# A planner's spare time behind the landing of projection weights, and the bytes it counts for a gate's rows

## The chip, the cores and the metric

The kernel runs on one core of a Trainium2 chip. The metric is the device time of one execution in microseconds (us), taken as the median of several runs. A profile of one execution shows what each engine did: PE (matrix products, with PEld for its weight loads), ACT, DVE and POOL (elementwise work), and SP, which here issues nearly every DMA.

## What is computed

One decoder block on 1024 tokens of width 1024, float32:

```python
mod = silu(c) @ w_ada + b_ada                    # 6 x 1024: shift, scale, gate for each half
h = rms_norm(x, g_attn_pre) * (1 + sc_a) + sh_a
proj = h @ w_in                                  # q, k, v of two mixers; part of q and k is rotated
oa = banded_attention(qa, ka, va, 127, sink)     # mixer A: 8 query heads on 2 key heads, window 128
ob = dilated_mixture_attention(qb, kb, vb)       # mixer B: 8 heads, three dilated windows
mixed = concat(rms_norm(oa, g_mix_a), rms_norm(ob, g_mix_b))
x = x + gt_a * rms_norm(mixed @ w_out, g_attn_post)
h = rms_norm(x, g_mlp_pre) * (1 + sc_m) + sh_m
x = x + gt_m * rms_norm(square(relu(h @ w_up)) @ w_down, g_mlp_post)
```

`gt_a` and `gt_m` are the two gates: one row of 1024 numbers each.

## The kernel before

**Products in three parts.** Each float32 operand is split into a high part (a cast on ACT) and a low part (a subtraction on DVE or POOL), and each product is three matrix products: high by high, high by low, low by high (L920, L921, L923 for the projections).

**Units.** The projection's columns are cut into six units, numbered 0 to 5 (two for mixer A, four for mixer B). A unit has three column groups `c` of 128, two halves `x` of the tokens, and eight slices `k` of the depth. Its weights come as six tiles of 128 x 512 floats (256 KB). Unit 0 is loaded in a fixed order during the start. For units 1 to 5 ("from unit two on", counted from one) `next_unit_w` makes, for each tile, a load (`load_w`, L541, tile `w_st`, two buffers) and a split (`split_w`): the cast on ACT (L550, into `w_hl`, six buffers) and the subtraction on DVE or POOL (L555), which gives the raw buffer back. Tiles one and two hold the first column group's slices 0 to 3 and 4 to 7, tiles three and four the second group's, five and six the third's. The next unit's loads are made when the second half of the unit before begins.

**Attention.** While units 1 to 5 are projected, the attention of the heads that are ready runs beside them: scores on PE (`s_ps`, L1203 and L1258), row minima on DVE (`mn`, L1222 and L1273), exponentials on ACT (`p_sb`, L1229 and L1278), a reciprocal on DVE (`den`), the normalisation on POOL or ACT (L1234, L1290), transposes on PE (`pt_ps`), the split of the transposed probabilities (`ph`, L1322 on ACT and L1326 on DVE), the product with v on PE (`o_ps`, L1338 to L1350). Projected q and k go out of `hl` into `qt` and `kt` by DMAs issued on SP (L863). After the attention come the output projection (`y_ps`) and the MLP (`mlp_ps`).

**Gates.** `ada_piece` makes pieces of the later modulation rows: it loads slices of `w_ada` (`wa_st`), accumulates them on POOL (24 pieces beside the attention) or DVE (8 pieces in the MLP), and after each fourth piece sums over the partitions on PE (`ada_ps`). For a gate (g = 0, 1 beside the attention, g = 6, 7 in the MLP) it also loads two rows of 512 floats, each broadcast to all 128 partitions (`f_gl`, L1112 and L1113, tile `gate_st`), then adds and multiplies on DVE (L1118, L1124 or L1126) and stores the gate (L1128).

**The planner.** The order on each engine is not left to a queue at run time. While the program is built, `Sched.run` places every step with a counted duration: at each turn it takes, over all engines, the step that can start first. On one engine ties go to the lower priority number; among DMAs on SP what counts first is also the start, then the priority (stores of q and k −12, weight tiles −10 to −9.5, modulation pieces 20, a gate's rows 19). The instructions are emitted in that order, and at run time each engine goes through its own in order, each waiting for its semaphores. What the planner counts is thus no waiting time of its own; it only decides who stands behind whom.

A load on SP counts as follows: it occupies SP for 0.62 us, enters one DMA queue (`dma`) no sooner than 1.1 us after its start, takes `nbytes / 345e3` us of it, and has landed 0.8 us later. A step on another engine that needs it is ready at that time plus the load's `slack`. Until now `slack` was 3.0 us for loads of priority 15 to 24 while the projections run (`SLACK`, set to 0 when the output projection opens) and 0 for all others; the same spare time is also added to the start of such a load.

Of the kernel before, what the change touches and what calls it, by code (L numbers as in the profile page):

```python
# [134 lines left out]
def lat(a, b):  # L135

    if a == "PE" or b == "PE":
        return 0.2
    return 0.06 if a == "POOL" else 0.14
# [38 lines left out]
class Sched:  # L178
# [21 lines left out]
    def op(self, eng, dur, emit, deps=(), **kw):  # L200

        o = self.step(dur, emit, deps, **kw)
        o.alts = None
        if isinstance(eng, str):
            self.queue[eng].append(o)
        else:
            o.alts = dict(zip(eng, zip(dur, emit)))
            for e in eng:
                self.queue[e].append(o)
        return o.ev  # L210
# [7 lines left out]
    def ready(self, o, e):  # L218
        t = 0.0
        for d in o.deps:  # L220
            if d.t is None:
                return None
            x = d.t + lat(d.eng, e) + (0.0 if e == "SP" else d.slack)
            if x > t:
                t = x
        for r, n in o.takes:
            if n == 0:
                continue
            if len(r.free) < n:
                return None  # L230
            x = sorted(r.free)[n - 1]
            if x > t:
                t = x
        return t + self.spare(o) if e == "SP" else t

    def spare(self, o):

        return self.slack if 15 <= o.prio < 25 else 0.0

    def give_out(self, e, o, start):  # L240
        dur, emit = o.alts[e] if o.alts else (o.dur, o.emit)
# [91 lines left out]
def t_as(n):  # L333
    return 0.2 + 0.00083 * n


def t_dv(n):
    return 0.066 + 0.00104 * n
# [19 lines left out]
def hybrid_block(ctx: ExitStack, tc: tile.TileContext, x, positions, w_ada, b_ada, g_attn_post, w_in, w_out,  # L358
# [7 lines left out]
    op, pe_op = sc.op, sc.pe_op  # L366
# [27 lines left out]
    r_stg, r_w, r_wst, r_hl = Res(5), Res(WR), Res(WS), Res(0)  # L394
# [60 lines left out]
    def stage(name):  # L455
        if st.stgp is None:
            return ring_r(name)
        return st.stgp.tile([P, 1024], F32, name=name, tag="stg")

    def load(emit, nbytes, deps=(), takes=(), prio=5, gives=(), after=None, n=1):  # L460
        return op("SP", nbytes / (345e3 if prio > -500 else 370e3), emit, deps, takes=takes, prio=prio, gives=gives, after=after, n=n)

    def rsqrt_mean(dst, src, dep):
        box = []
# [36 lines left out]
    def in_turn(emit, nbytes, ring):  # L501

        before, mine = gone[0], Ev()
        gone[0] = mine

        def issued():
            mine.t = 0.0
        return load(emit, nbytes, [before], takes=[(ring, 1)], prio=pri(), after=issued)

    e_c = load(lambda: nc.sync.dma_start(head[:], consts[:, 0:HEAD]), 106496, prio=pri())  # L510
    wa_t, wa_e = {}, {}

# [23 lines left out]
    w_raw, w_rawe, w_hl, w_e = {}, {}, {}, {}  # L536

    def load_w(u, i, prio=None, deps=()):
        def emit():
            t = w_raw[u, i] = prp.tile([P, 512], F32, name="w_st", tag="w_st", bufs=WS)  # L540
            nc.sync.dma_start(t[:], w_in[6 * u + i])  # L541
        if prio is None:
            w_rawe[u, i] = in_turn(emit, 262144, r_wst)
        else:
            w_rawe[u, i] = load(emit, 262144, deps, takes=[(r_wst, 1)], prio=prio)

    def split_w(*a):
        def hi():
# [15 lines left out]
    for a, n in order0:  # L564
        if a == "x":
            load_x(n)
        elif a == "w":
            load_w(0, n)
        else:
            load_ada(a, n)  # L570
# [12 lines left out]
    e = op("ACT", 0.1, lambda: A.activation(cond[:], c_raw, AF.Exp, scale=-1.0), [e_c], prio=0)  # L583
# [32 lines left out]
    e = op("DVE", 4.2, f_turns, [e_pos, e_c], prio=1)  # L616

    def f_sin():
# [5 lines left out]
                prio=1)  # L624
# [150 lines left out]
    def tables_b():  # L775
# [12 lines left out]
       prio=8)  # L788
# [200 lines left out]
    def next_unit_w(u, deps=()):  # L989
        if u + 1 < 6:  # L990
            for i in range(6):
                load_w(u + 1, i, prio=-10 + i / 10, deps=deps)
                split_w(u + 1, i)
# [54 lines left out]
    def ada_piece(i, eng, accp, psum, r_ps, r_acc=None):  # L1048
# [9 lines left out]
        def f_acc():  # L1058
# [3 lines left out]
            for j in range(2):  # L1062
# [8 lines left out]
        e = op("DVE" if eng is V else "POOL", 1.2 if eng is V else 4.1, f_acc,  # L1071
               [el, ada.e], takes=[(r_acc or r_adacc, 1)] if jp == 0 else [], gives=[(r_stg, 1)], prio=9)
# [19 lines left out]
        if row and g > 5:  # L1092
# [7 lines left out]
            def f_al(eng):  # L1100
                return lambda: eng.tensor_tensor(hl[0][:, 1], acc[0][:, :512], hl[0][:, 0].bitcast(F32), ALU.subtract)
            e = op("ACT", t_as(512), f_ah, [e], takes=[(r_stg, 1)], prio=4)
            ada.e = e
            e = op("DVE", t_dv(512), f_al(V), [e], gives=[(r_acc or r_adacc, 1)], prio=4)
        ef = pe_op("fin", (0.46 if g > 5 else 0.86) if row else 0.45, f_fin, [e], takes=[(r_ps, 1)],
                   gives=[(r_stg if row and g > 5 else r_acc or r_adacc, 1)])
        if row:
            gate, gp = (gate_d[0], g_attn_post) if g < 2 else (gate_d[1], g_mlp_post)

            def f_gl():  # L1110
                ada.gate[g] = t = stage("gate_st")
                nc.sync.dma_start(t[:, 0:512], b_ada[0:1, col:col + 512].to_broadcast([P, 512]))  # L1112
                nc.sync.dma_start(t[:, 512:1024], gp[0:1, n0:n0 + 512].to_broadcast([P, 512]))  # L1113
            eg = load(f_gl, 524288, [e], takes=[(r_stg, 1)], prio=19)

            def f_g1():
                t = ada.gate[g]
                V.tensor_tensor(t[:, 0:512], b[0][:, :512], t[:, 0:512], ALU.add)  # L1118
            e1 = op("DVE", t_dv(512), f_g1, [ef, eg], gives=[(r_ps, 1)], prio=4)

            def f_g2():
                t = ada.gate[g]
                if g < 2:
                    V.tensor_tensor(t[:, 0:512], t[:, 0:512], t[:, 512:1024], ALU.mult)  # L1124
                else:
                    V.scalar_tensor_tensor(t[:, 0:512], t[:, 0:512], D ** 0.5, t[:, 512:1024], ALU.mult, ALU.mult)  # L1126
            e2 = op("DVE", t_dv(512), f_g2, [e1], prio=4)
            e_mod[g] = load(lambda: nc.sync.dma_start(gate[:, n0:n0 + 512], ada.gate[g][:, 0:512]), 262144, [e2],  # L1128
                            gives=[(r_stg, 1)], prio=18)
        else:  # L1130
            k0 = n0 // P

            def f_c():
                if g < 4:
                    V.tensor_tensor(s_m[:, k0:k0 + 4], b[0][:, 0:4], cols[:, 40 + k0:44 + k0], ALU.add)
                else:
                    V.tensor_tensor(g_m[:, k0:k0 + 4], b[0][:, 0:4], b1m[:, k0:k0 + 4], ALU.add)
                    V.tensor_tensor(g_m[:, k0:k0 + 4], g_m[:, k0:k0 + 4], cols[:, 16 + k0:20 + k0], ALU.mult)
            e_mod[g] = op("DVE", 0.15, f_c, [ef], gives=[(r_ps, 1)], prio=4)

    def feed_ada():
        if st.d > 1.0 + ada.i * 4.1 / NADA and ada.i < NADA:
            ada_piece(ada.i, G, lambda: adp.tile([P, 512], F32, name="ada_acc", tag="ada_acc", bufs=1), lambda: px.tile([P, 512], F32, name="ada_ps", tag="x"), r_x)
            ada.i += 1
        return ada.i == NADA
# [1052 lines left out]
    def feed_ada2():  # L2198
        if ada.i < 32:
            if ada.i >= NADA and ml.begun > 8 + 2 * (ada.i - NADA):  # L2200
                ada_piece(ada.i, V, lambda: stage("ada_acc"),
                          lambda: px.tile([P, 512], F32, name="ada_ps", tag="x"), r_x, r_stg)
                ada.i += 1
            return False

        def f_gate():
            ml.gate = ring_r("gate_m")
            nc.sync.dma_start(ml.gate[:], gate_d[1][:])
        ml.e_gate = load(f_gate, 524288, [e_mod[6], e_mod[7]], takes=[(r_h2, 1)], prio=17)
        return True  # L2210
# [32 lines left out]
```

## Time and profile before

| | us |
|---|---|
| median of 3 runs (lowest, highest) | 1120.49 (1119.75, 1122.23) |
| the profiled execution's own time | 1121.31 |
| its span in the profile | 1119.5 |
| PE busy | 1102.1 |
| DVE busy | 822.5 |
| ACT busy | 629.2 |
| POOL busy | 245.0 |

The page and the views of the trace give times from the start of the span. A row of a timeline has its start, its length, engine, line, operation, the tile written and the tile read; in square brackets stands how long the engine had been idle before it and what ended that. A row of the waits has the total, the number of times and the longest. SPq is SP's queue: the time there is what issuing took, and a DMA's way from issue to landing is given by the rows of DMA issues (count, size, median us).

### The profile page before, as it was taken

Reading aid. Unit: us, or ns where it says so; the run is one execution under the profiler, and the core shown is the slowest. Engines: PE = TensorE matmul, PEld = TensorE weight load, DVE = VectorE, ACT = ScalarE, POOL = GpSimd, SP = SyncE. Lnnn points to the kernel's source line nnn. Section 1 sums busy time; section 2 is a strip of 40 time slices with the busy share of each in tenths; the row PEclk is TensorE's granted clock in tenths of the full one; section 3 lists DMA queues with packets and bytes.
Section 4 is the critical chain, followed back from the end, with each engine's and each line's share of the span. In section 5 each row is a group of like instructions: output and inputs, shape, how many; then the busy total and the mean of one; then the engine's idle time right before and its main releaser. Section 6 shows DMA issues by size and latency. Waiting matters only on the chain.

```text
span 1119.5 us, 15561 instructions
## 1 busy us (share of the span) xinstructions
PE 1102.1 (98%) x5393; PEld 917.0 (82%) x5393; DVE 822.5 (73%) x1391; ACT 629.2 (56%) x1092; POOL 245.0 (22%) x313
## 2 busy tenths in 40 slices
PE   8999999999999999999999999999999999999996
PEld 7778787888888888888888888888888888888885
DVE  7868777666677676689798564798643996537998
ACT  8759776464665666576674335653154632247542
POOL 2158758657741231110000000000000000000003
PEclk9999999999999999999999999999999999999999
DMA  9766675554514643656761279521578113584104
GB/s 351 219 197 183 189 226 198 177 178 160 204 33 151 238 136 97 220 226 234 279 244 38 82 239 335 200 62 52 198 262 304 36 57 111 190 316 154 39 19 150
DMA packets 94110, 195.39 MB, mean 175 GB/s; under 512 B 9008, under 2 KB 31664, under 8 KB 94032
## 3 DMA queue, kind: packets, MB, share of 16 engines
q1 hardware_dynamic: 94032, 194.40, 50.4%
q8 instruction: 43, 0.70, 0.2%
q14 instruction: 35, 0.29, 0.1%
HBM read 141.80 MB, written 33.03 MB: 156 GB/s over the span
## 4 chain that ended last, share of the span: by engine, by line
PE 84%; DVE 9%; issue 2%; ACT 2%; DMA 2%; POOL 0%; SPq 0%; DVEq 0%; POOLq 0%; ACTq 0%
PE mlp_ps L2056 17%; PE mlp_ps L2055 17%; PE mlp_ps L2057 17%; PE pj L920 4%; PE pj L923 4%; PE pj L921 4%; PE s_ps L1203 3%; PE y_ps L1609 2%; PE y_ps L1611 2%; PE y_ps L1610 2%; PE o_ps L1338 2%; PE pt_ps L1308 1%; PE o_ps L1350 1%; PE pt_ps L1311 1%; DVE hw L1819 1%
## 5 line engine op out<-in xcount | busy, mean ns | idle before, releaser
L2055 PE MATMUL mlp_ps<-hw 128*128 128x512 f32 x896 | 348.9, 389 | 0.2 <-DVE u L2092 0.2
L2057 PE MATMUL mlp_ps<-hw 128*128 128x512 f32 x896 | 348.6, 389 | 0.0
L2056 PE MATMUL mlp_ps<-hw 128*128 128x512 f32 x896 | 348.6, 389 | 0.0
L2055 PEld LDWEIGHTS mlp_ps<-hw 128*128 128x128 f32 x896 | 168.2, 188 | 35.8 <-DVE u L2092 0.6
L2057 PEld LDWEIGHTS mlp_ps<-hw 128*128 128x128 f32 x896 | 168.2, 188 | 35.0
L2056 PEld LDWEIGHTS mlp_ps<-hw 128*128 128x128 f32 x896 | 168.2, 188 | 34.6
L1819 DVE TENSOR_TENSOR hw<-w,hw 128x1024 fp32r<-128x1024 f32 x96 | 114.5, 1219 | 96.3 <-ACT hw L1812 96.1
L1812 ACT CAST hw<-w 128x1024 fp32r<-128x1024 f32 x96 | 97.7, 1048 | 126.9 <-PE mlp_ps L2057 86.2
L2165 POOL TENSOR_TENSOR st<-st,nhalf 128x1 f32<-128x1 f32 x8 | 8.0, 1011 | 591.8 <-DVE st L2163 591.8
L920 PE MATMUL pj<-hw,w_hl 128*128 128x512 f32 x240 | 101.7, 424 | 0.0
L923 PE MATMUL pj<-hw,w_hl 128*128 128x512 f32 x240 | 94.7, 394 | 0.0
L921 PE MATMUL pj<-hw,w_hl 128*128 128x512 f32 x240 | 94.4, 393 | 0.0
L1326 DVE TENSOR_TENSOR ph<-pt_ps,ph 128x512 fp32r<-128x512 f32 (+1 forms) x110 | 68.8, 646 | 29.3 <-ACT ph L1322 29.0
L1812 ACT CAST hw<-u 128x1024 fp32r<-128x1024 f32 x48 | 48.6, 1051 | 63.2 <-PE mlp_ps L2057 63.2
L1322 ACT CAST ph<-pt_ps 128x512 fp32r<-128x512 f32 (+1 forms) x110 | 58.1, 555 | 28.2 <-PE pt_ps L1311 24.5
L1819 DVE TENSOR_TENSOR hw<-u,hw 128x1024 fp32r<-128x1024 f32 x48 | 56.9, 1217 | 17.8 <-ACT hw L1812 17.8
L1229 ACT ACTIVATE p_sb<-p_sb,mn 128x128 f32<-128x128 f32 (+3 forms) x64 | 49.7, 776 | 32.2 <-DVE mn L1222 31.7
L1234 POOL TENSOR_SCALAR p_sb<-p_sb,den 128x128 f32<-128x128 f32 (+3 forms) x64 | 49.4, 778 | 77.3 <-DVE den L1232 65.2
L2113 DVE TENSOR_TENSOR yacc<-yacc,mlp_ps 128x512 f32<-128x512 f32 x96 | 62.0, 680 | 3.3 <-PE mlp_ps L2057 3.3
L1070 POOL TENSOR_TENSOR ada_acc<-ada_acc,wa_st 128x512 f32<-128x512 f32 x42 | 55.0, 1310 | 3.5
L923 PEld LDWEIGHTS pj<-hw,w_hl 128*128 128x128 f32 x240 | 45.1, 188 | 10.5
L1609 PE MATMUL y_ps<-hw,oh 128*128 128x512 f32 x128 | 52.0, 407 | 0.0
(215 smaller groups left out, 1972.6 us busy)
## 6 DMA issues: line engine op xcount, KB each, us to landing
hw<-s_dram SPq DMA_DIRECT2D x84, 512.0 KB, 4.3
wa_st<-in_w_ada SPq DMA_DIRECT2D x32, 512.0 KB, 4.7
w<-in_w_up SPq DMA_DIRECT2D x32, 512.0 KB, 5.5
w<-in_w_down SPq DMA_DIRECT2D x32, 512.0 KB, 6.9
s_dram<-hw SPq DMA_DIRECT2D x28, 512.0 KB, 3.8
qt<-hl SPq DMA_DIRECT2D x40, 256.0 KB, 2.7
w_st<-in_w_in SPq DMA_DIRECT2D x36, 256.0 KB, 2.8
x_sb<-in_x SPq DMA_DIRECT2D x16, 512.0 KB, 5.5
```

The lines of the kernel that those rows point to most:

```text
L920: T.matmul(ps, w[:, 0, n], h[0], start=(k == 0), stop=False)
L921: T.matmul(ps, w[:, 1, n], h[0], start=False, stop=False)
L923: T.matmul(ps, w[:, 0, n], h[1], start=False, stop=(k == KC - 1))
L1322: A.copy(b["ph"][:, 0, :w], b["pt"][:, :w])
L1326: V.tensor_tensor(b["ph"][:, 1, :w], b["pt"][:, :w], b["ph"][:, 0, :w].bitcast(F32), ALU.subtract)
L1609: T.matmul(ps[:], b["oh"][:, k], wh[:, c0:c0 + 512], start=(k == 4 * m), stop=False)
L1812: A.copy(out[j][0], flat(src[j]))
L1819: V.tensor_tensor(out[j][1], flat(src[j]), out[j][0].bitcast(F32), ALU.subtract)
L2055: T.matmul(ps[m][:], sh, mh, start=starts and k == 0, stop=False, **kw)
L2056: T.matmul(ps[m][:], sh, ml_, start=False, stop=False, **kw)
L2057: T.matmul(ps[m][:], sl, mh, start=False, stop=k == 3, **kw)
L2113: e = op("DVE", t_dv(512), lambda: V.tensor_tensor(y(), y(), ps[m][:], ALU.add), [e, ml.e_y[tb, n]], gives=gives, prio=1)
```

## The change

Weight tiles of units 1 to 5 get the kind `"w"`. A load of that kind gets a `slack` of 2.5 us: the cast that needs it is ready, in the planner's count, 2.5 us after the counted landing. The load's own start is not delayed. And a gate's rows, 524288 bytes, are counted as 1152000 bytes: 3.34 us of the counted DMA queue instead of 1.52.

```diff
-        return t + self.spare(o) if e == "SP" else t
+        return t + self.spare(o) if e == "SP" and o.kind != "w" else t
...
-        return self.slack if 15 <= o.prio < 25 else 0.0
+        return self.slack if 15 <= o.prio < 25 else 2.5 if o.kind == "w" else 0.0
...
-    def load(emit, nbytes, deps=(), takes=(), prio=5, gives=(), after=None, n=1):
-        return op("SP", nbytes / (345e3 if prio > -500 else 370e3), emit, deps, takes=takes, prio=prio, gives=gives, after=after, n=n)
+    def load(emit, nbytes, deps=(), takes=(), prio=5, gives=(), after=None, n=1, kind=""):
+        return op("SP", nbytes / (345e3 if prio > -500 else 370e3), emit, deps, takes=takes, prio=prio, gives=gives, after=after, n=n, kind=kind)
...
-            w_rawe[u, i] = load(emit, 262144, deps, takes=[(r_wst, 1)], prio=prio)
+            w_rawe[u, i] = load(emit, 262144, deps, takes=[(r_wst, 1)], prio=prio, kind="w")
...
-            eg = load(f_gl, 524288, [e], takes=[(r_stg, 1)], prio=19)
+            eg = load(f_gl, 1152000, [e], takes=[(r_stg, 1)], prio=19)
```

## The prediction

> **What bounds the kernel now.** I read the page first, then busy time by stretch, then what TensorE (PE) waited for while the projections and the attention run (60 to 480 us).
>
> ```profile
> span 1119.5 us, 15561 instructions
> PE 1102.1 (98%) x5393; PEld 917.0 (82%) x5393; DVE 822.5 (73%) x1391; ACT 629.2 (56%) x1092; POOL 245.0 (22%) x313
> ...
> 40.00:560.00 520.00, 515.14 (x2780) 432.63 (x2779) 385.12 (x866) 338.39 (x686) 221.76 (x276) 1.00 0.55 185
> 560.00:1080.00 520.00, 520.00 (x2295) 430.48 (x2294) 371.79 (x392) 244.53 (x325) 0.00 (x0) 1.00 0.45 158
> 1080.00:1119.50 39.50, 31.00 (x137) 25.34 (x135) 32.91 (x57) 12.89 (x29) 10.59 (x10) 0.95 0.29 107
> ```
>
> In the three stretch rows the columns are length, then PE, PEld, DVE, ACT, POOL busy, granted clock, DMA share, GB/s. PE is the bound: idle 4.86 us from 40 to 560, nothing in the MLP (560 to 1080), 8.5 us in the tail. An order of steps can therefore win only what PE idles in the first stretch. Those waits are:
>
> ```profile
> PE s_ps L1258 <- DVE mn L1273: 1.6, 1, 1.6
> PE o_ps L1350 <- DVE ph L1326: 0.8, 2, 0.6
> PE o_ps L1338 <- DVE ph L1326: 0.6, 2, 0.3
> PE o_ps L1350 <- ACT ph L1322: 0.5, 1, 0.5
> PE pm_o L1581 <- DVE o_sb L1575: 0.4, 1, 0.4
> PE s_ps L1203 <- DVE mn L1222: 0.3, 1, 0.3
> PE s_ps L1258 <- DMA qt<-hl: 0.2, 1, 0.2
> ```
>
> They add up to 4.4 us, and 1.6 of it is one wait. The timelines around it, all engines:
>
> ```profile
> 59.77 4.95 SPq L541 DMA_DIRECT2D w_st<-in_w_in  x3
> 65.63 1.38 SPq L863 DMA_DIRECT2D kt<-hl  x2
> 72.36 4.58 SPq L863 DMA_DIRECT2D qt<-hl  x6
> 77.00 0.58 SPq L541 DMA_DIRECT2D w_st<-in_w_in  x1
> ...
> 81.00 0.62 ACT L550 CAST w_hl<-w_st 128x512 fp32r<-128x512 f32 x1 [2.31 <-DMA w_st<-in_w_in]
> 81.70 1.29 POOL L555 TENSOR_TENSOR w_hl<-w_st,w_hl 128x512 fp32r<-128x512 f32 x1 [2.10 <-ACT w_hl L550]
> 83.14 0.18 DVE L1282 RECIPROCAL den<-den 128x4 f32<-128x4 f32 x1 [2.40 <-ACT p_sb L1278]
> 83.42 1.84 POOL L1290 TENSOR_SCALAR p_sb<-p_sb,den 128x256 f32<-128x256 f32 x4 [0.43 <-DVE den L1282]
> 84.16 0.75 PE L1258 MATMUL s_ps<-kt,qt 128*128 128x256 f32 x4 [1.58 <-DVE mn L1273]
> 84.75 0.40 PE L920 MATMUL pj<-hw,w_hl 128*128 128x512 f32 x1
> ```
>
> The sixth weight tile of unit 1 is issued at 77.00. ACT reaches its step (the cast, L550) at 81.00 − 2.31 = 78.69 and stands there. Behind it in ACT's order are the four exponentials that DVE's reciprocal needs (2.40 late), behind that reciprocal are the row minima, and for those PE's next scores wait 1.58. The same thing at the end of unit 2's weights:
>
> ```profile
> 77.00 3.98 DMA w_st<-in_w_in
> 120.97 5.59 DMA w_st<-in_w_in
> ...
> 117.63 1.41 SPq L1112 DMA_DIRECT2D gate_st<-in_b_ada  x1
> 120.97 0.54 SPq L541 DMA_DIRECT2D w_st<-in_w_in  x1
> 126.64 0.62 ACT L550 CAST w_hl<-w_st 128x512 fp32r<-128x512 f32 x1 [1.77 <-PE pt_ps L1315]
> 125.92 0.69 DVE L1124 TENSOR_TENSOR gate_st<-gate_st 128x512 f32<-128x512 f32 x1 [0.78 <-DMA gate_st<-in_g_attn_post]
> 127.80 0.49 PE L1350 MATMUL o_ps<-ph,v_hl 128*128 128x512 f32 x1 [0.52 <-ACT ph L1322]
> 128.52 0.50 PE L1350 MATMUL o_ps<-ph,v_hl 128*128 128x512 f32 x1 [0.23 <-DVE ph L1326]
> ...
> gate_st<-in_b_ada SPq DMA_DIRECT2D x1, 256.0 KB, 5.6
> gate_st<-in_g_attn_post SPq DMA_DIRECT2D x1, 256.0 KB, 6.4
> ```
>
> The first two rows are from the chain of waits: 3.98 and 5.59 us from issue to landing. The ACT row at 126.64 names PE, but the tile landed at 126.56, so its 1.77 us are the DMA's. The copies of the probabilities (ph) stand behind it, and PE waits 0.52 and 0.23 for them.
>
> **The change part by part.** No instruction is added or removed and no byte more is moved. What changes is the times that the planner counts, and by them the order on each engine's queue.
>
> *The 2.5 us behind weight tiles.* The planner counts a tile as landed 1.1 + 262144/345e3 + 0.8 = 2.66 us after its issue when the queue is free; 3.98 and 5.59 were taken. Now the cast is placed no sooner than 5.16 us after the issue, and steps that are ready earlier go ahead of it. At 77.00 that suffices (5.16 > 3.98): the exponentials start at 78.69 instead of 81.53, the reciprocal's inputs are there by about 80.7, the minima follow, and PE, which without its wait would come at 84.16 − 1.58 = 82.58, finds its bank free. Gain 1.58. If the tile landed late again, the cast would stand in its new place and as much could be lost there; the slowest landing of the 36 says how far that goes:
>
> ```profile
> DMA to landing us min/median/max: 2.4/2.8/6.7
> ```
>
> At 120.97, 5.59 is 0.43 more than 5.16; the gate covers that.
>
> *The gate's bytes.* 1152000/345e3 = 3.34 us of counted queue time, where 524288 gave 1.52: everything counted behind a gate's rows moves by up to 1.82 us. The rows were issued from 117.63, the second part (after 1.41 us of issue, so at about 119.0) landed 6.4 us later, at 125.4, 7.8 us after the first issue. Counted with its spare 3.0 it was 6.42, and is 8.24 now: DVE's 0.78 at 125.92 goes. The tile at 120.97 is counted right behind the gate, so its cast moves by up to 2.5 + 1.82 = 4.3, more than the 1.77 it was early. Gain 0.52 + 0.23 = 0.75. Gates two to four: the second one's rows are issued at 155.62 and first used at 174.42, some 19 us later (rows below), so nothing. The last two lie in the MLP, where no spare is counted; their sums and the store of the gate move by 1.82, and SP stands at that store already:
>
> ```profile
> 155.62 0.53 SPq L1112 DMA_DIRECT2D gate_st<-in_b_ada  x1
> 174.42 0.69 DVE L1118 TENSOR_TENSOR gate_st<-ada_ps,gate_st 128x512 f32<-128x512 f32 x1
> ...
> SPq L1128 <- DVE gate_st L1126: 6.4, 2, 3.4
> ```
>
> Behind it on SP are loads of MLP operands. PE's 520.00 of 520.00 us is the cover; I take nothing. Without the cover it could cost, or give back, 3.4 us a gate.
>
> *What the 2.5 us push back.* There are two raw buffers for weight tiles, so a cast placed 2.5 us later lets the tile after next be issued 2.5 us later. On SP that decides at one place. The third of the DMAs at 59.77 (tile five of unit 1) is issued at about 59.77 + 4.95 − 0.33 = 64.4, some 1.2 us ahead of the stores that begin at 65.63. 2.5 us later it meets them, and SP takes stores (priority −12) ahead of weights (−9.6) as long as any is ready. They last until 72.36 + 4.58 = 76.94. So tiles five and six go out together, at about 77.0 and 77.6, instead of 64.4 and 77.0. Who waits for tile five is PE's third column group of unit 1, which begins with the row at 84.75, and so at 83.17 once the 1.58 is gone. Tile five lands near 81.0, ACT comes to it about then (78.69 + 2.5 = 81.2), its 0.62 and POOL's 1.29 end at 83.1: just in time, with POOL's normalisations (1.84 at 83.42) competing. I charge 0.5 us, between 0 and 1.58; it is nearest to the 0.52 that PE waited behind a held-up ACT at 127.80. Below nothing would be another order that packs better; the 0.61 of the wait at 181.01 (below) is what that could give.
>
> For the other tiles of units 2 to 5 I expect no move of their own: there ACT's cast starts after a matmul group has freed a slot, or with the tile long landed, and none but the two above waited for a DMA.
>
> *New order, same work.* Every shift changes which of two ready steps goes first, also far behind it. One place shows what a bad neighbour costs:
>
> ```profile
> 178.58 1.77 DVE L555 TENSOR_TENSOR w_hl<-w_st,w_hl 128x512 fp32r<-128x512 f32 x1 [0.56 <-ACT w_hl L550]
> 178.52 1.28 POOL L1070 TENSOR_TENSOR ada_acc<-ada_acc,wa_st 128x512 f32<-128x512 f32 x1
> 181.01 0.50 PE L1350 MATMUL o_ps<-ph,v_hl 128*128 128x512 f32 x1 [0.61 <-DVE ph L1326]
> ```
>
> DVE's subtraction began 0.06 us after a POOL sum and took 1.77 us, ending about 0.55 after POOL did at 179.80; PE then waited 0.61. The Trainium skill (SBUF — State Buffer, Who interferes with whom) says that a DVE instruction with two SBUF inputs contends with a GpSimd instruction that reads SBUF, and that the later one is blocked, not slowed; this trace agrees, 1.77 against a POOL instruction of 1.28.
>
> **Sum.** −1.58 − 0.52 − 0.23 + 0.5 = −1.8 us against the profiled execution's own 1121.31 (span 1119.5 and 1.8 around it), so 1119.5 there. That execution is 0.8 above the median 1120.49, so the forecast for the median is 1118.7, −0.16%. A measurement of this kernel can tell about 0.2%, 2.24 us, from no change: the borders are 1118.25 and 1122.73.
>
> **The rivals.** *Cleaner than I charge* (faster): tile five costs nothing, and one or two of the other waits (0.61 at 181.01; 0.6 before L1338) go in the new order. −2.33 − 0.6 = −2.9 gives 1117.6; all 4.4 us gone give 1116.1, the floor. For it: DVE, ACT and POOL have slack in the whole stretch (385, 338, 222 of 520). Against: a new order makes waits as well as taking them.
>
> *PE waits for tile five* (slower): if the pair, sent out together into a queue that has just taken the stores, takes 6.7 us like the slowest tile instead of 3.98, it lands at 83.7, 2.5 us behind ACT's 81.2; with one lot of POOL's normalisations (1.84) ahead of its subtraction PE stands 2.5 + 1.84 = 4.3 us at the row of 84.75, with two 6.2, and scores and transposes stand behind it in PE's order. −2.33 + 4.3 to 6.2 is +2.0 to +3.9; the middle gives 1123.4. It decides from a tile ready 2.33 us later than PE wants it, from where on the change loses; each us beyond is a us of PE. For it: the margin worked out above is 0.1 us. Against: PE's own order is planned with the same 2.5 us, so other PE work is put ahead.
>
> *The waits only move* (no change): ACT no longer stands at the cast but DVE or PE waits for another late transfer; all 2.3 us come back, 1120.5. For it: the smaller waits, seven sources that nothing here touches, are what a different order leaves.
>
> *Subtractions meet POOL*: the moved tile steps fall on DVE beside a POOL sum twice more, each for 0.61 of PE: −1.8 + 1.2 = −0.6, 1119.9. This is the skill's rule of above as a mechanism of this kernel.
>
> **Chances.** The forecast 0.36, its spread putting 0.08 of that below 1118.25; cleaner 0.26; the waits only move 0.12; subtractions meet POOL 0.06; tile five late, with any other order that loses over 2.24 us, 0.20. Faster 0.08 + 0.26 = 0.34, same 0.28 + 0.12 + 0.06 = 0.46, slower 0.20. The range goes from the floor 1116.1 to the slower rival's 1123.4; the forecast's own range is 1117.6 to 1119.9.
>
> **What would show it.** Right: in the new timeline no ACT cast L550 of units 1 and 2 with a wait of over 0.5 us on w_st; PE's longest wait between 60 and 480 us well under 1.58; PE busy from 40 to 560 up by about 1.8 of a stretch as long as before; two w_st issues in a row near 77; PE busy all of the MLP. Wrong: PE's pj rows waiting for w_hl (L550 or L555) near 83 to 88, a sum of PE waits as large as 4.4 again from other sources, or any PE idle time in the MLP behind a gate's steps.

## The result and the profile after

The changed kernel takes 1117.73 us (median of 10 runs, 1116.71 to 1118.85); the kernel before 1120.78 (10 runs, 1119.75 to 1122.23). By the medians that is 3.05 us faster; the ratio is 0.9969 with an interval of 0.9962 to 0.9977, 0.31%, more than the 0.2% that a measurement can tell from no change. The forecast was 1118.7, within 0.2% as its likeliest class; the time lies 1 us below it, at the price of the rival "cleaner than I charge" (1117.6). The medians here and below leave out two executions, one of `slack15` and one of `slack_u1_g1`, which took two and three times as long as the rest.

The profile's page after, and busy time by stretch (length, then PE, PEld, DVE, ACT, POOL busy, granted clock, DMA share, GB/s):

```profile
span 1114.9 us, 15568 instructions
PE 1100.7 (99%) x5393; PEld 917.0 (82%) x5393; DVE 819.5 (74%) x1388; ACT 630.3 (57%) x1092; POOL 247.9 (22%) x316
...
40.00:560.00 520.00, 518.09 (x2800) 436.70 (x2799) 386.25 (x867) 341.25 (x688) 225.02 (x279) 1.00 0.56 188
560.00:1080.00 520.00, 520.00 (x2296) 430.56 (x2295) 369.87 (x390) 243.55 (x323) 0.00 (x0) 1.00 0.44 155
1080.00:1114.90 34.90, 26.40 (x117) 21.54 (x115) 30.44 (x54) 11.75 (x28) 10.59 (x10) 0.95 0.32 121
```

PE is idle 1.91 us from 40 to 560 us, where it was idle 4.86; the MLP is full, and the tail idles 8.5 us as before. What PE waited for from 60 to 480 us, after (total, times, longest):

```profile
PE pm_o L1581 <- DVE o_sb L1575: 0.4, 1, 0.4
PE s_ps L1258 <- DMA qt<-hl: 0.4, 1, 0.4
PE o_ps L1338 <- DVE ph L1326: 0.3, 1, 0.3
PE s_ps L1203 <- DVE mn L1222: 0.3, 1, 0.3
```

1.4 us in place of 4.4. Both waits for late tiles are gone (1.58 near 84 us, 0.52 and 0.23 near 128), and so are three that the prediction's sum left standing, near 181, 204 and 209 us (0.61, 0.11 and 0.25). From 75 to 108 us PE idled 1.58 us before, from 108 to 131 0.75, from 131 to 213 0.97; now it idles in none of the three. Outside them it idles much as before (0.52 us from 40 to 75, where it was 0.22; 1.39 from 213 to 560, where it was 1.35): the whole gain is made between 84 and 213 us. The two profiled executions differ by more than the medians, 4.16 us, as before's (1121.31) was above its median and after's (1117.15) below.

SP's queue in the new order, and the rows of ACT, POOL and DVE where the waits had been:

```profile
66.06 3.85 SPq L863 DMA_DIRECT2D qt<-hl  x6
70.00 0.53 SPq L541 DMA_DIRECT2D w_st<-in_w_in  x1
70.62 1.31 SPq L863 DMA_DIRECT2D kt<-hl  x2
71.98 5.40 SPq L863 DMA_DIRECT2D qt<-hl  x6
77.44 0.58 SPq L541 DMA_DIRECT2D w_st<-in_w_in  x1
...
81.52 0.61 ACT L550 CAST w_hl<-w_st 128x512 fp32r<-128x512 f32 x1
...
179.43 1.28 POOL L555 TENSOR_TENSOR w_hl<-w_st,w_hl 128x512 fp32r<-128x512 f32 x1
180.32 0.94 DVE L555 TENSOR_TENSOR w_hl<-w_st,w_hl 128x512 fp32r<-128x512 f32 x1 [0.65 <-ACT w_hl L550]
```

Tile six of unit 1 goes out as late as before (77.44; 77.00 before), but its cast at 81.52 has no bracket: ACT did other work until the tile was there. Tile five goes out at 70.00, in a gap among the stores, not after all of them. The subtraction of unit 3's fourth tile, which took DVE 1.77 us beside a POOL sum near 178, is now POOL's own (1.28 us at 179.43). DVE's row at 180.32 is the fifth tile's; it starts 0.89 us behind POOL's and takes 0.94, and no wait of PE follows.

### The profile page after: what moved, and what is told of

The parts are those of the page before. It is cut to its first block, busy times and chain, and to the rows that moved or that the text cites. A ratio compares the mean times of both kernels' runs of the same rounds, so it can differ in the third digit from the quotient of the medians.

```text
span 1114.9 us, 15568 instructions
## 1 busy us (share of the span) xinstructions
PE 1100.7 (99%) x5393; PEld 917.0 (82%) x5393; DVE 819.5 (74%) x1388; ACT 630.3 (57%) x1092; POOL 247.9 (22%) x316
## 4 chain that ended last, share of the span: by engine, by line
PE 85%; DVE 7%; DMA 3%; issue 2%; ACT 1%; SPq 0%; POOL 0%; POOLq 0%; DVEq 0%; ACTq 0%
PE mlp_ps L2057 17%; PE mlp_ps L2055 17%; PE mlp_ps L2056 17%; PE pj L920 5%; PE pj L923 5%; PE pj L921 4%; PE s_ps L1203 3%; PE y_ps L1609 2%; PE y_ps L1611 2%; PE y_ps L1610 2%; PE o_ps L1338 2%; DMA wa<-in_w_ada 2%; PE pt_ps L1308 1%; PE s_ps L1258 1%; PE o_ps L1350 1%
```

## The experiments

Theory one: the gain is the two waits for late tiles. Rivals: it comes from elsewhere in the new order; or the halves of the change each do a part. All kernels were timed against the kernel before in the same session (its medians there: 1120.82 to 1121.34), and differences in us are between those medians.

**One cast moved by hand, nothing planned anew.** This takes the kernel before and emits the split of unit 1's sixth tile later by five ACT steps; the other steps of each engine keep their order.

```diff
-        emit()
+        place(self, e, o, emit)          # holds a named step back by n steps of its engine
...
+MOVES = {'split15': ('ACT', 5)}          # tile six of unit 1
```

> The order of the kernel before, with one step moved: the cast of the sixth weight tile of unit 1 stands five ACT steps later (behind six exponentials instead of one), and its subtraction on POOL right behind the first normalisation. PE, DVE and SP have the same order as before. Late-tile theory (a cast that stands on a late tile holds up what is behind it on ACT, and PE waits for that): PE's wait near 84 goes and is not given back, 1.6 to 1.7 us faster than before; the waits near 127, 181 and 208 stay. Rival (the gain lies in the new order of everything behind it): 0 to 0.5 us faster, another wait takes the place.

1119.48 us, ratio 0.9986 (0.9977 to 0.9995): 1.3 us faster by the medians, 1.6 by the ratio. The cast, and PE's scores that had waited 1.58 at 84.16, in this kernel:

```profile
82.05 0.60 ACT L550 CAST w_hl<-w_st 128x512 fp32r<-128x512 f32 x1
...
83.03 0.63 PE L1258 MATMUL s_ps<-kt,qt 128*128 128x256 f32 x4
```

Neither waits. In its profiled execution PE's projection rows stand 0.6 us behind before's up to this place (82.34; 81.73 before) and 1.2 ahead of them from it on (83.51; 84.75 before). The prediction's main term thus goes with a single step.

The median is not the price of that wait alone, however. The wait of 0.52 near 128 us is not in this kernel's list of waits either: its tile, issued at 119.48, was there for a cast at 123.67, 4.2 us later and not 5.59. And part of the lead is given back in the MLP (last section). Nor has the wait one size: in `gate_only` and `slack_u2on` below, where the cast keeps its place, PE waits 1.35 and 1.05 here.

**The same at the second place, and the collision.** `split24` is tile five of unit 2 (near 127 us); `split33` is the subtraction that met POOL near 178, put behind three DVE steps.

```diff
-MOVES = {'split15': ('ACT', 5)}
+MOVES = {'split15': ('ACT', 5), 'split24': ('ACT', 2)}                         # mv15_24
+MOVES = {'split15': ('ACT', 5), 'split24': ('ACT', 2), 'split33': ('DVE', 3)}  # mv_all
```

> As the kernel with the sixth tile of unit 1 moved, and also the cast of the fifth weight tile of unit 2 two ACT steps later, behind the two copies of the probabilities. Late-tile theory: PE's waits near 84 and 127 go, 2.6 to 2.9 us faster than before, nearly all of the change's 3.05. Rival: 0 to 1 us faster.

> As the kernel with two casts moved, and also the subtraction of the fourth weight tile of unit 3 three DVE steps later, behind two subtractions of the probabilities and a reciprocal, so that it does not begin beside a POOL sum with PE's operand behind it. Collision theory (the DVE subtraction of 1.77 us beside POOL's sum cost PE its 0.61 to 0.77 near 181): 0.5 to 0.8 us faster than the kernel with two casts moved, 3.2 to 3.6 faster than before. Rival: the subtraction meets another POOL step or PE waits elsewhere, no difference to the kernel with two casts moved.

1119.16 (0.9983, 0.9974 to 0.9992) and 1118.84 (0.9980, 0.9971 to 0.9989). Each step adds 0.3 us by the medians, in the right direction but less than an interval can part; the late-tile theory had 2.6 to 2.9 us for the first of the two kernels, the collision theory 3.2 to 3.6 for the second, and both missed. The wait that the second step was to take away, 0.52, was already absent from `mv15`. The third step does what it should in the trace: PE's 0.61 near 179 (0.66 in `mv15_24`) is gone. Three steps moved by hand give 2.0 us of the 3.05.

**The halves of the change.** `slack_only` keeps the 2.5 us and counts the gates as before; `gate_only` the reverse; `slack_u1` and `slack_u2on` give the 2.5 us to unit 1 alone and to units 2 to 5 alone, gates as before.

```diff
 # slack_only, from the changed kernel
-            eg = load(f_gl, 1152000, [e], takes=[(r_stg, 1)], prio=19)
+            eg = load(f_gl, 524288, [e], takes=[(r_stg, 1)], prio=19)
...
 # slack_u1 (slack_u2on: u > 1), the same and
-            w_rawe[u, i] = load(emit, 262144, deps, takes=[(r_wst, 1)], prio=prio, kind="w")
+            w_rawe[u, i] = load(emit, 262144, deps, takes=[(r_wst, 1)], prio=prio, kind="w" if u == 1 else "")
```

> The 2.5 us behind all weight tiles of units 1 to 5, a gate's rows counted as before (524288). Late-tile theory: both of PE's waits near 84 and 127 go, 2.4 to 3.1 us faster than before, as the whole change. Gate theory (from the 4.2 us that PE stood at the transposes of v behind the second gate's sum when only unit 1 had the 2.5 us; both use one PSUM bank): whether that wait comes depends on whether the order puts the gate's column sum ahead of a transposition of v; here v goes ahead of it, so none. Rival (the gate's rows are late wherever they are not counted at 3.34): 1 to 4 us slower than before.

> A gate's rows counted as 1152000 bytes, no spare time behind weight tiles. The casts that stood on late tiles keep their places on ACT. Late-tile theory: PE's waits near 84 and 127 stay, no difference to before within 0.7 us. Rival (the gate's count takes away the wait near 127 by itself): 0.8 to 1.3 us faster.

> The 2.5 us only behind the weight tiles of unit 1 (units 2 to 5 and the gates are counted as before); the planner makes a new order from unit 1 on. Late-tile theory: the wait near 84 goes (1.6 to 1.7), the one near 127 comes back where the fifth tile of unit 2 still lands late: 1.5 to 2.0 us faster. Rival (new order): as fast as the whole change, 2.7 to 3.3 us.

> The 2.5 us only behind the tiles of units 2 to 5, gates as before. PE and SP have the order of before; on ACT one cast near 126 and one near 135 move behind a few steps. Late-tile theory: the wait near 84 stays, those near 127 (0.52 and 0.23) go: 0.7 to 1.2 us faster than before. Rival: moving that cast brings nothing, as it brought only 0.3 us between the kernels with one and with two casts moved: 0 to 0.4 us.

| kernel | us | ratio (interval) | against before |
|---|---|---|---|
| whole change | 1117.73 | 0.9969 (0.9962 to 0.9977) | -3.05 |
| slack_only | 1126.72 | 1.0048 (1.0034 to 1.0062) | +5.5 |
| gate_only | 1120.60 | 0.9998 (0.9990 to 1.0007) | none |
| slack_u1 | 1124.93 | 1.0034 (1.0021 to 1.0046) | +4.1 |
| slack_u2on | 1120.69 | 0.9994 (0.9985 to 1.0003) | none |

The halves do not add: the one loses 5.5, the other gives nothing, both together win 3. In `gate_only` PE's longest waits are still there, the one near 84 us, one of 0.69 near 131 and the 0.61 of the collision near 181:

```profile
PE s_ps L1258 <- DVE mn L1273: 1.4, 1, 1.4
PE o_ps L1350 <- DVE ph L1326: 1.3, 2, 0.7
```

PE's longest waits in the two that lose, `slack_only` first:

```profile
PE o_ps L1350 <- ACT ph L1322: 5.4, 1, 5.4
PE pm_o L1581 <- DVE o_sb L1575: 0.4, 1, 0.4
PE s_ps L1258 <- DMA qt<-hl: 0.3, 1, 0.3
```

```profile
PE pv L891 <- DVE gate_st L1118: 4.2, 1, 4.2
PE pm_o L1581 <- DVE o_sb L1575: 0.4, 1, 0.4
PE s_ps L1258 <- DMA qt<-hl: 0.4, 1, 0.4
```

In both, the late-tile waits are gone (for `slack_u1` only the one near 84 us was expected to go), and one new long wait stands behind them. Where it comes from in `slack_only`, by the timeline:

```profile
147.08 6.44 POOL L1290 TENSOR_SCALAR p_sb<-p_sb,den 128x256 f32<-128x256 f32 x12
156.42 1.26 POOL L1070 TENSOR_TENSOR ada_acc<-ada_acc,wa_st 128x512 f32<-128x512 f32 x1
...
157.71 0.69 ACT L834 ACTIVATE hl<-pj,head 128x512 fp32r<-128x512 f32 x1 [6.99 <-POOL ada_acc L1070]
158.30 1.06 ACT L1322 CAST ph<-pt_ps 128x512 fp32r<-128x512 f32 x2
158.93 1.70 PE L1350 MATMUL o_ps<-ph,v_hl 128*128 128x512 f32 x2 [5.42 <-ACT ph L1322]
```

ACT's evacuation of a projection tile (L834) needs a staging buffer that POOL gives back with its accumulation; POOL has a run of twelve normalisations to do first. ACT stands 6.99 us, and the casts of `ph` that PE needs stand behind it. And in `slack_u1`:

```profile
155.44 1.02 PE L1088 MATMUL ada_ps<-ada_acc,ones 128*128 128x512 f32 x2
161.26 0.43 SPq L1112 DMA_DIRECT2D gate_st<-in_b_ada  x1
168.38 0.69 DVE L1118 TENSOR_TENSOR gate_st<-ada_ps,gate_st 128x512 f32<-128x512 f32 x1 [4.23 <-issue]
169.12 1.12 PE L891 MATMUL pv<-head,vt 128*128 128x128 f32 x4 [4.16 <-DVE gate_st L1118]
...
gate_st<-in_b_ada SPq DMA_DIRECT2D x1, 256.0 KB, 7.0
```

The second gate's sum lies in a PSUM bank that the transposes of v (`pv`) need next, and DVE empties it only when the gate's rows have landed, 7.0 us after their issue. In the changed kernel the rows go out 7.5 us earlier, and `pv` stands ahead of the sum, so nothing waits:

```profile
153.74 0.47 SPq L1112 DMA_DIRECT2D gate_st<-in_b_ada  x1
157.60 0.60 PE L891 MATMUL pv<-head,vt 128*128 128x128 f32 x4
160.82 1.02 PE L1088 MATMUL ada_ps<-ada_acc,ones 128*128 128x512 f32 x2
```

**Is that one wait the loss?** `so_mv6` is `slack_only` with the evacuation (and its low part and stores) held back by six ACT steps.

```diff
+MOVES = {'ev201': ('ACT', 6)}            # unit 2, first half, second column group
```

> The kernel is slack_only (the spare time for every unit, the gates counted as before), with one step held back by hand and nothing planned anew: the evacuation of unit 2's second projection tile of the first half (ScalarE, line 834), with its low part and its stores, goes out six ScalarE steps later, so that the two casts of ph that stood behind it go first. PE's order stays that of slack_only. Theory one (the 5.5 us that slack_only lost are one wait, ScalarE's 6.99 us idle for a staging buffer that GpSimd gives back late, and the slow clock after it): no wait of o_ps on ph over 1 us, mean clock back from 0.994 to 0.998, time 1117.5 to 1121, a gain of 0 to 3.5 on before. Rival (slack_only's order is late as a whole, the wait is only where it shows): another wait of 3 us or more within 15 us behind it (on the projection's bank, on vt or on p_sb), time 1123 or more.

1122.21, ratio 1.0008 (0.9999 to 1.0016). Between the two theories: 0.9 us over before, so 4.6 of the 5.5 us are gone, so the wait and what followed it were most of the loss. But a shorter one took its place, this time on the bank that the held evacuation frees:

```profile
158.83 0.62 PE L920 MATMUL pj<-hw,w_hl 128*128 128x512 f32 x1 [1.90 <-DVE hl L837]
```

The buffer comes back at 157 us whoever asks for it; holding one step back moved the queue behind it and did not cure it.

**Which gate's count matters.** `slack_u1_g1` is `slack_u1` with the larger count for the second gate alone, `slack_g0` the changed kernel with it for the first gate alone.

```diff
-            eg = load(f_gl, 1152000, [e], takes=[(r_stg, 1)], prio=19)
+            eg = load(f_gl, 1152000 if g == 1 else 524288, [e], takes=[(r_stg, 1)], prio=19)  # slack_u1_g1
+            eg = load(f_gl, 1152000 if g == 0 else 524288, [e], takes=[(r_stg, 1)], prio=19)  # slack_g0
```

> The 2.5 us behind the tiles of unit 1 alone, as in the kernel that was 4 us slower than before, and of the gates only the second one's rows counted as 1152000 bytes. Its column sum on PE still goes ahead of the transposes of v that share its PSUM bank, but these are placed 2.7 us later. Gate theory: PE's wait of 4.2 us shrinks to under 1.6, and the slow clock behind it goes with it: 4 to 6 us faster than the kernel with unit 1's spare time alone, 0.5 to 2 us faster than before. Rival (the slow kernel lost its time elsewhere): within 1 us of it.

> The changed kernel with the larger count for the first gate's rows alone; gates two to four are counted as before. It parts the interaction: slack_only (no gate counted larger) lost 5.5 us, the whole change won 3. Theory one (it is the first gate's count that turned the order, well ahead of where slack_only stood still): the planned order on PE is that of the changed kernel but for some rows in the MLP, with the transposes into the shared bank ahead of the second gate's sum; so 1117 to 1119 us, 2 to 4 under before, and no wait of PE of over 0.5 us between 60 and 480 us. Rival (the second gate's rows have to be counted at their 7 to 8 us of service, or DVE's sum stands and holds the shared bank): a wait at DVE's sum L1118 near 160 us of 2 to 4 us that reaches PE, time 1121 to 1125.

`slack_u1_g1`: 1123.36, 2.1 over before, ratio 1.0018 (1.0009 to 1.0028). That is better than `slack_u1`, but not the 0.5 to 2 us under before that the gate theory had. The rows of PE's two long waits:

```profile
170.56 0.66 PE L891 MATMUL pv<-head,vt 128*128 128x128 f32 x4 [2.29 <-DVE gate_st L1118]
175.66 1.19 PE L1350 MATMUL o_ps<-ph,v_hl 128*128 128x512 f32 x4 [1.90 <-DVE v_hl L902]
```

The larger count shortened the first (4.16 to 2.29): PE comes to `pv` 3.3 us later, and the rows go out at 161.99, where they went at 161.26. But the sum still stands ahead of `pv`, and a second wait follows. `slack_g0`: **1117.47**, ratio 0.9966 (0.9954 to 0.9978), the whole gain. Its waits of PE:

```profile
PE pm_o L1581 <- DVE o_sb L1575: 0.4, 1, 0.4
PE s_ps L1258 <- DMA qt<-hl: 0.3, 1, 0.3
PE o_ps L1338 <- DVE ph L1326: 0.3, 1, 0.3
PE s_ps L1203 <- DVE mn L1222: 0.3, 1, 0.3
PE pv L891 <- ACT vt L885: 0.2, 1, 0.2
```

So the counts of gates two to four are worth nothing that can be measured here, and the first gate's is worth 9 us beside the spare time (from +5.5 to -3.6). It does so at a distance: its rows go out near 118 us, and the wait that it avoids lies near 155. That the first gate's rows are counted truly where they are used is not what pays; alone (`gate_only`) all four counts gave nothing. It shifts the order behind it to one without a long wait; by which steps, the runs don't show.

**Other amounts of spare time.**

```diff
-        return self.slack if 15 <= o.prio < 25 else 2.5 if o.kind == "w" else 0.0
+        return self.slack if 15 <= o.prio < 25 else 1.5 if o.kind == "w" else 0.0  # slack15; 5.0 in slack5
```

> The changed kernel with 1.5 us of spare time in place of 2.5. Theory one (each count makes a new order behind it, and what decides is whether that order holds a long wait): its planned order has the second gate's rows go out at the same place as the changed kernel, but the sum with them ahead of the transposes into the same PSUM bank by only 1.0 us (in the changed kernel the transposes stand 5 us ahead of the sum), so it holds PE there for 0 to 2 us; without that wait 1117.5 to 1119.5, with it up to 1123. Rival, the spare time by its size (1.5 us is too little for a tile that landed 1.6 to 2 us late near 84 us): a wait of PE near 84 of 0.5 to 1 us and a time of 1118 to 1119.5, whatever the order behind.

> The changed kernel with 5.0 us of spare time in place of 2.5. Theory one (new order, and what it happens to hold): the planned order has the sum with the second gate's rows 0.95 us ahead of the transposes into the same bank, as in slack_u1 (0.75), and its tiles' splits a good deal later; 1117.5 if no wait of over 1 us stands in it, 1121 to 1126 if one does. Rival, the spare time by its size: all tiles are counted late enough, so it is at least as good as 2.5 us, 1116.5 to 1118.5.

1118.23 (0.9968, 0.9957 to 0.9980) and 1119.09 (0.9979, 0.9971 to 0.9988). With 1.5 us the gate's rows go out early, and DVE's sum did not wait for them:

```profile
154.03 0.59 SPq L1112 DMA_DIRECT2D gate_st<-in_b_ada  x1
163.19 0.68 DVE L1118 TENSOR_TENSOR gate_st<-ada_ps,gate_st 128x512 f32<-128x512 f32 x1
```

No wait of PE is over 0.54, and none stands near 84 us, where the rival expected one; the time can't be told from that of 2.5 us. With 5.0 us there is no long wait either, and it gains less by the medians, though the intervals touch. Both kernels keep the second gate's sum ahead of the transposes, as `slack_u1` does (152.64 and 164.09 in `slack15`, 157.22 and 165.19 in `slack5`, whose rows go out at 154.37), and PE does not wait there. So it is not the place of the sum alone that cost PE 4.16 us in `slack_u1`, but that place together with rows that went out late. With the gates counted larger, all three amounts give an order without a long wait; with the gates as before, 2.5 us gave one with it.

## Why the prediction came out as it did

**The bound and the place: right.** PE sets the time, only its idle time between 40 and 560 us could be won, and it was: 4.86 to 1.91 us, the MLP and the tail as they were.

**The term of 1.58: right in its cause, and shown** by `mv15`; the wait itself measured 1.05 to 1.58 where it stood, and the medians of `mv15` (1.3 to 1.6) hold more than it. **The terms of 0.52 and 0.23**: gone in the changed kernel; `mv15_24` measured 0.3 beside `mv15`, too little to part from nothing. How late that tile lands changes with the order (4.2 us at most in `mv15`, 5.59 before).

**The charge of +0.5 for tile five: mis-sized; it was 0.** The step that failed is "they last until 76.94, so tiles five and six go out together". The stores are not ready without a break: tile five went out at 70.00 in between, and its cast ran at 74.79. That puts the sum at -2.3; with the three waits of the next paragraph it is -3.3, against 3.05 measured.

**"For the other tiles of units 2 to 5 I expect no move of their own": half right.** Spare time for these units alone gave nothing measurable (`slack_u2on`). But the order changed there together with all else: the waits near 181, 204 and 209 us went, 0.97 us in all, of which the collision near 178 is one (`mv_all`, 0.3 by the medians). The prediction had this as its "cleaner" rival. That rival's price, 1117.6, is what came; the forecast's working had given the new order no gain. That the three went and no new one came is luck, as far as the forecast goes. Why these three waits went, and whether that would hold for another order, the runs don't settle: they went also in `slack_only`, `slack_u1` and `slack_g0`, while waits as large stayed in `gate_only` and `slack_u2on`; so it is with unit 1's spare time that they go.

**Gates two to four cost nothing: right, shown by `slack_g0`.** But the reason given, 19 us between the second gate's issue and its use, belonged to the old order. In the changed kernel it is 9 us (153.74 to 162.71), still enough. In `slack_u1` the sum stands so that DVE waits for these very rows and PE 4.16 us behind it.

**What the prediction missed** is the interaction. It summed wait by wait, -1.58 and -0.75, as if the rest of the order stood, and it saw no need of both halves together. Measured, they are +5.5 and 0 alone. Its slower rival was tile five arriving late; that did not happen in any run. The slower outcome that was near is another one: a step that holds a shared buffer (a staging buffer, a PSUM bank) put ahead of what PE needs. The list of waits before could not show it, since no such wait stood there: its transposes near 160 us (160.39) stand 13 us ahead of the second gate's sum (173.37).

**What would show it**: four of the five signs came (no cast with a wait on its tile in units 1 and 2, PE's longest wait 0.4, PE busy up by 2.95 where 1.8 was expected, PE full in the MLP). Two tile issues in a row near 77 did not.

## What to carry to other kernels

Where a program plans the order ahead from counted times, a changed count is not a local edit: it draws a new order for everything behind it, and what that order is worth (here from -3 to +5.5 us) has to be read from its waits, not summed from the wait that one set out to remove. To find what one wait is worth, move that one step by hand and keep the rest, and read along PE's rows where the lead is won and where it is lost again: the median alone holds both. A step that holds a scarce buffer until a transfer lands should stand behind the work that needs the buffer next, or the transfer be issued well ahead.

## What the runs showed of the hardware

**A long wait of PE costs more than its length.** After the waits of `slack_u1`, `slack_only` and `so_mv6`, by stretch in that order (the granted clock is third from the end):

```profile
169.00:172.00 3.00, 2.88 (x9) 2.50 (x10) 2.89 (x6) 0.60 (x2) 0.58 (x1) 0.50 1.04 387
172.00:175.00 3.00, 3.00 (x12) 2.44 (x12) 2.54 (x5) 1.41 (x3) 2.83 (x4) 0.65 0.32 122
```

```profile
159.00:162.00 3.00, 2.88 (x6) 1.99 (x7) 2.99 (x11) 0.96 (x3) 0.00 (x0) 0.50 0.66 216
162.00:165.00 3.00, 3.00 (x15) 2.40 (x15) 0.68 (x1) 2.12 (x7) 0.00 (x0) 0.80 0.92 307
```

```profile
160.00:165.00 5.00, 5.00 (x22) 3.99 (x22) 1.08 (x3) 1.33 (x3) 1.39 (x4) 0.75 0.76 236
```

The clock falls to half and is back some 3.5 to 5 us after PE resumes. At half clock a matmul row of 0.39 us reads 0.63, and such rows start 0.43 us apart, not 0.23; in `slack_u1` eight of them cost 1.6 us beyond the wait of 4.2. The threshold isn't sharp: no such stretch follows the 1.58 us in the kernel before (clock 1.00 from 84 to 95), one follows the 1.90 us of `so_mv6`, and none the first wait (2.29) of `slack_u1_g1`, though one did its second (0.61 from 176 to 180). Nor is every execution alike: of `so_mv6`'s eleven, six have a mean clock of 0.996 and take 1122.2 to 1123.4 us, five have 0.997 or 0.998 and take 1120.6 to 1122.0. The Trainium skill (TensorE: Matmul & The Clock Gate, Part 1: The HAM clock gate) states half clock after an idle window of about 3.4 us, and that the window runs free. The 0.50 agrees; that 1.90 us of visible wait sufficed in one case is shorter than that window.

**PE's cover in the MLP is thin at one place.** In `mv15`, where nothing near it was changed, a late piece of modulation weights reached PE:

```profile
653.84 1.54 DVE L1067 SCALAR_TENSOR_TENSOR ada_acc<-wa_st,cond,ada_acc 128x512 f32<-128x512 f32 x2 [3.75 <-DMA wa_st<-in_w_ada]
656.42 0.69 DVE L1101 TENSOR_TENSOR acc_hl<-ada_acc,acc_hl 128x512 fp32r<-128x512 f32 x1
657.17 0.50 PE L1086 MATMUL ada_ps<-acc_hl,ones_h 128*128 128x512 f32 x1 [0.59 <-DVE acc_hl L1101]
```

The matmul of this row and its twin ahead of it (656.08) start 1.09 us apart. PE had come here with a lead: the first matmul of the MLP starts at 495.56 in `mv15` and at 497.91 before, 2.35 us earlier, and the first behind this place at 657.50 and 658.76, only 1.26 earlier. `mv15_24`, `mv_all`, `gate_only` and `slack_u2on` lose 0.25 to 0.5 us against before at the same place, in one profiled execution each. The changed kernel and `slack_g0` lose nothing there. So the kernels with steps moved by hand give back here part of what they won, and some of the 1 us that they leave open against the whole change may lie in it; the runs don't part that.
